# Attention in a decoder trunk: the products of probabilities and values in fp32r parts

## The chip, the core and the metric

The kernel runs on one core of a Trainium2 chip. The metric is the device time of one execution in microseconds, the median over runs. A core has five engines, each of which takes its own instructions in order: TensorE (PE in the profile, with its weight loads as PEld), VectorE (DVE), ScalarE (ACT), GpSimd (POOL), and SyncE (SP), which here only issues DMAs. They wait for one another through semaphores. Operands lie in SBUF; matmuls write into PSUM banks, from which VectorE and ScalarE read.

## The reference

Two layers on a sequence of 1024 positions of width 1024, all in fp32. Layer 0 ("even") has a mixer of two parts, a chunked gMLP and an attention with 8 heads of 64 channels; layer 1 has a gated linear attention; each layer ends with a gated MLP with a causal convolution. The change lies in the attention of layer 0, of which the kernel computes two branches: a causal band of the 128 positions before a query (window 128, dilation 1), and queries and keys strided by 4, with the third branch (dilation 16) folded into the masks of the second. Cut to what matters:

```python
def dilated_branch(q, k, v, window, dilation):      # blocks of 128 positions of one residue
    ...
    s = jnp.einsum('bhrnic,bhrnjc->bhrnij', qb, kk) * (hd ** -0.5)
    s = jnp.where(valid, s, NEG)
    m = jnp.max(s, -1, keepdims=True)
    p = jnp.exp(s - m)
    den = jnp.sum(p, -1)
    o = jnp.einsum('bhrnij,bhrnjc->bhrnic', p, vv) / den[..., None]
    lse = m[..., 0] + jnp.log(den)
```

The branches are then weighted by a softmax over their `lse`, and heads are put side by side.

## The kernel before

**Numbers.** TensorE multiplies in two formats here: fp32, and fp32r, a rounded form of it. For most products the kernel splits each fp32 operand into two fp32r parts, the rounded value (high) and the rest (low), and adds three products of parts. `split` (L98) makes the parts: ScalarE casts the high one (L100), VectorE subtracts it from the source for the low one (L101). `scaled` (L103) does the same with a factor on the source (L105, L106). The products of probabilities and values are plain fp32 matmuls in this kernel.

**The even mixer** starts with the transposed, split input `hq`, which all projections read. The attention runs in four passes of two heads each (`p` = 0 to 3). `project` (L694) does for each of eight tiles of 128 positions (`n`): the projection to queries, keys and values (24 matmuls of 384 columns into a bank `pj`, of which there are two), norms of queries and keys (VectorE, ScalarE, GpSimd), the scaled values `vN` (L718, ScalarE; three buffers), which also go to DRAM (`vd`), the transposes of the queries (`tq`) and keys (`tk`) with their copies, and then one `unit` (L668) of the first branch. Behind the eight tiles the values are read back in strided order (`v4`). `dilated` (L755) does eight such units on strided queries and keys (a quarter of the positions each, in two blocks).

A **unit** handles one block of 128 queries, two heads `s`, and one or two blocks `j` of keys. For each head: scores in a bank `sc` (L659, fp32r), the mask and the extremum in one VectorE instruction (L664), the exponential on ScalarE (L665), and a transpose of each block of probabilities on TensorE into a bank `pts` (L679). Then all blocks are copied to SBUF (`pT`), on ScalarE in odd units (L682) and on VectorE in even ones (L684), and multiplied by the values into `po` (L687):

```python
            for s in range(2):
                for j in range(nj):
                    T.matmul(po[:, i, 64 * s : 64 * s + 64], pT[:, s, j, :], vb[j][:, 64 * s : 64 * s + 64],
                             start=(j == 0), stop=(j == nj - 1))
```

`po` is one bank that takes four units, 128 columns each, and is then copied to `ot` by ScalarE (L747, L766). `combine` and `combined` weigh the branches by VectorE and GpSimd.

**Order.** Instructions are placed engine by engine by a scheduler at build time, which moves them across tiles and passes: the strided units of one pass stand among the projections of the next, and the gMLP's value and gate projections (`pv`, `pu`) among those of the last. Which instruction waits for which follows from buffers: a tile's buffer is reused when its last reader is done.

**Weights.** The projection's weights come as raw fp32 rows and are split into parts (`load_qkv`, L565), eight tiles to a pass. Passes 0 and 2 take four of them from a pool of their own, `wx`, with four buffers, and four from the pool `wp` with eight, which all other stages use too; passes 1 and 3 take all eight from `wp`.

Of the kernel before, what the change touches and what calls it, by code (L numbers as in the profile page):

```python
# [9 lines left out]
F32 = mybir.dt.float32  # L10
# [45 lines left out]
def trunk(ctx: ExitStack, tc: tile.TileContext, a, out):  # L56
# [452 lines left out]
    def even(gm_open):  # L509
        with ExitStack() as st:  # L510
# [6 lines left out]
            par0 = ExitStack()  # L517
            wx = par0.enter_context(tc.tile_pool(name="wx", bufs=4, side="right", reuse_waits="tile"))
            pq0 = par0.enter_context(tc.tile_pool(name="pq0", bufs=1, side="right", reuse_waits="tile"))
# [45 lines left out]
    def load_qkv(p, wx):  # L565

        ws = []
        for kp in range(4):
            raw = load_raw(a["w_qkv"][p, kp], f"wq{p}{kp}r", 768)
            for i in range(2):  # L570
                k = 2 * kp + i
                src, gain = raw[:, i * 384 : i * 384 + 384], g0[:, k : k + 1]
                if p % 2 or k >= 4:
                    ws.append(parts_of(src, f"wq{p}{kp}_{i}", gain=gain))
                else:
                    w = wx.tile([P, 2, 384], F32R, tag="wx", name=f"wx{p}{k}")
                    ws.append([w[:, j, :] for j in range(2)])
                    scaled(ws[-1], src, gain)
        return ws
# [61 lines left out]
    def attention(ps, at, av, pq, pq0, par0, wx, wq0, masks, gm_open):  # L641
# [26 lines left out]
        def unit(p, name, i, ot, po, qv, kv, vb, mask, wide=lambda t: t):  # L668


            nj = len(vb)
            W = nj * P
            pts = ps.tile([P, 2, nj, P], F32, tag="pt", name="pP" + name)
            for s in range(2):
                sm = scores(p, f"{name}{s}", qv(s), lambda part: kv(s, part), W,
                            mask[:, 2 * P - W :],
                            ot[:, i, 128 + s : 129 + s], ot[:, i, 130 + s : 131 + s], wide)
                for j in range(nj):
                    T.transpose(pts[:, s, j, :], sm[:, j * P : j * P + P], ident)  # L679
            pT = at.tile([P, 2, 2, P], F32, tag="pT", name="pT" + name)  # L680
            if i % 2:
                A.copy(pT[:, :, :nj, :], pts)  # L682
            else:
                V.tensor_copy(pT[:, :, :nj, :], pts)  # L684
            for s in range(2):
                for j in range(nj):
                    T.matmul(po[:, i, 64 * s : 64 * s + 64], pT[:, s, j, :], vb[j][:, 64 * s : 64 * s + 64],  # L687
                             start=(j == 0), stop=(j == nj - 1))

        def outputs(name):  # L690
            return (at.tile([P, 4, 132], F32, tag="ot", name="ot" + name, bufs=5),
                    ps.tile([P, 4, P], F32, tag="po", name="po" + name))

        def project(p, ws=None, then=None):  # L694
# [5 lines left out]
            kT = pool.tile([P, 4, S], F32R, tag="kT", bufs=1, name=f"kT{p}")  # L700
            vd = dram.tile([S, P], F32, name=f"vd{p}")
            vN, os = [], []
            for n in range(NT):
# [12 lines left out]
                G.tensor_tensor(qn, qn, gqk, op=ALU.mult)  # L716
                vN.append(pq.tile([P, P], F32, tag="vN", bufs=3, name=f"vN{p}{n}"))
                A.mul(vN[n], pj[:, 256:384], rn)  # L718
                Q.dma_start(rows(vd, n), vN[n])
                qs = pq.tile([P, 2, P], F32R, tag="qs", bufs=2, name=f"qs{p}{n}")  # L720
# [18 lines left out]
                if n % 4 == 0:  # L739
                    ot, po = outputs(f"{p}n{n}")  # L740
                    os.append(ot)
                m0 = max(n - 1, 0)
                unit(p, f"{p}n{n}", n % 4, ot, po, lambda s, qT=qT: qT[:, s],
                     lambda s, i: kT[:, 2 * s + i, :].rearrange("p (r m) -> p r m", r=4)[:, :, 32 * m0 : 32 * n + 32],
                     vN[m0 : n + 1], mband, lambda t: t.rearrange("p (m r) -> p r m", r=4))
                if n % 4 == 3:
                    A.copy(ot[:, :, :P], po)  # L747
                if then and n in (3, 4):
                    then(n - 3)
            v4 = av.tile([P, 4, 2, P], F32, tag="v4", name=f"v4{p}", bufs=1)  # L750
            for b in range(2):
                Q.dma_start(v4[:, :, b, :], vd.rearrange("(b m r) c -> b m r c", b=2, r=4)[b])
            return os, qR, kT, v4

        def dilated(p, qR, kT, v4):  # L755

            od = dram.tile([S, 132], F32, name=f"od{p}")
            for g in range(2):
                ot, po = outputs(f"{p}d{g}")
                for i in range(4):  # L760
                    r, b = 2 * g + i // 2, i % 2
                    at0 = r * 256
                    unit(p, f"{p}d{g}{i}", i, ot, po, lambda s: qR[:, s, at0 + b * P : at0 + b * P + P],
                         lambda s, part: kT[:, 2 * s + part, at0 : at0 + b * P + P],
                         [v4[:, r, j, :] for j in range(b + 1)], mboth)
                A.copy(ot[:, :, :P], po)  # L766
                for b in range(2):
                    Q.dma_start(od.rearrange("(b m r) c -> b m r c", b=2, r=4)[b][:, 2 * g : 2 * g + 2, :],
                                ot.rearrange("p (r b) c -> p r b c", b=2)[:, :, b, :])
# [508 lines left out]
```

## Time and profile before

| | us |
|---|---|
| median of three runs | 2185.39 |
| lowest and highest run | 2182.70, 2185.51 |
| the profiled execution | 2186.67 |
| its span, first to last instruction | 2185.0 |
| of that, to the first matmuls of the output projection (the even mixer) | 388.7 |
| granted TensorE clock, mean over the span | 0.996 |

A line of a view that groups instructions reads: line of the kernel, engine, operation, output <- inputs by the program's names, shape, number of instructions | busy time and mean duration in ns | idle time of the engine just ahead of them, with what ended it. A line of a view by windows has, for each engine, its busy time in that stretch and the number of instructions in brackets, then the granted clock, the DMA engines' busy share and what they moved. In a timeline a line is a run of like instructions: start and length in us, engine, instruction, count. An operation whose line is a helper's is told apart by its tile.

### The profile page before, as it was taken

To read this page: it belongs to the slowest core of one execution; us is meant where nothing else is said; L and a number is where in the kernel's file an instruction comes from. 1 tells how busy PE (TensorE), PEld (TensorE's weight loads), DVE (VectorE), ACT (ScalarE), POOL (GpSimd) and SP (SyncE) were. 2 spreads that over 40 slices of the span, in tenths; PEclk is the share of its full clock that TensorE was granted. 3 is DMA by queue.
4 is the path that set the end of the run, shared out by engine and by line. 5 is a ranking of instruction groups with operands and counts; after the bars stand their busy time and mean duration, and the time that the engine had idled before them with its cause. 6 is when DMAs were issued, how large, how long until landed. Compare 5 with 4: busy or idle time off the path is not lost.

```text
span 2185.0 us, 29867 instructions
## 1 busy us (share of the span) xinstructions
PE 2145.9 (98%) x10508; PEld 1817.9 (83%) x10508; DVE 1538.2 (70%) x2459; ACT 1032.7 (47%) x1998; POOL 488.4 (22%) x519
## 2 busy tenths in 40 slices
PE   8999999999999999999999999999999999999999
PEld 7999988778888888888889887878788888888887
DVE  6566655567888888755576777666787879885554
ACT  6455545355444444444454455524544444444443
POOL 4444411013242434100010011100233524320000
PEclk9999999999999999999999999999999999999999
DMA  4122212655445444675553222377544444557555
GB/s 162 43 81 63 73 50 83 217 198 194 162 155 164 158 165 159 196 271 198 196 202 123 68 97 97 116 265 248 193 160 150 158 159 159 164 178 271 204 196 202
DMA packets 157254, 349.59 MB, mean 160 GB/s; under 512 B 17408, under 2 KB 54272, under 8 KB 156720
## 3 DMA queue, kind: packets, MB, share of 16 engines
q1 hardware_dynamic: 157104, 347.68, 47.5%
q8 instruction: 83, 1.36, 0.3%
q14 instruction: 67, 0.55, 0.1%
HBM read 239.02 MB, written 108.59 MB: 159 GB/s over the span
## 4 chain that ended last, share of the span: by engine, by line
PE 70%; DMA 4%; DVE 3%; ACT 1%; issue 1%; SPq 0%; POOL 0%; DVEq 0%; ACTq 0%
PE puB L290 11%; PE pgB L290 11%; PE pgC L290 5%; PE puC L290 5%; PE pdB L397 5%; PE pdC L397 5%; PE pv L190 4%; PE pdO L397 4%; PE puA L290 3%; PE pgA L290 3%; PE po L190 2%; PE pdQ L397 2%; PE pdP L397 2%; PE pBq L990 2%; PE pBr L990 2%
## 5 line engine op out<-in xcount | busy, mean ns | idle before, releaser
L101 DVE TENSOR_TENSOR da<-ar,da 128x512 fp32r<-128x512 f32 x154 | 106.4, 691 | 155.3 <-ACT da L100 155.2
L100 ACT CAST da<-ar 128x512 fp32r<-128x512 f32 x154 | 95.9, 622 | 209.4 <-PE pdC L397 91.3
L190 PE MATMUL po<-wo,hq 128*128 128x512 f32 x768 | 186.4, 398 | 0.6 <-DVE hq L101 0.3
L190 PEld LDWEIGHTS po<-wo,hq 128*128 128x128 f32 x768 | 143.3, 190 | 30.9 <-DVE hq L101 1.2
L190 PE MATMUL pv<-wv,hq 128*128 128x512 f32 (+2 forms) x768 | 139.9, 340 | 2.1 <-DVE b L1022 1.6
L397 PE MATMUL pdB<-dw,da 128*128 128x512 f32 x528 | 136.3, 391 | 0.6 <-ACT dw L100 0.6
L397 PE MATMUL pdC<-dw,da 128*128 128x512 f32 x528 | 135.9, 390 | 0.0
L190 PEld LDWEIGHTS pv<-wv,hq 128*128 128x128 f32 x768 | 119.0, 189 | 17.4 <-DVE b L1022 2.1
L190 PE MATMUL pj<-wq,hq 128*128 128x384 f32 x576 | 118.1, 348 | 0.0
L397 PEld LDWEIGHTS pdB<-dw,da 128*128 128x128 f32 x528 | 98.7, 188 | 21.9 <-ACT dw L100 1.0
L397 PEld LDWEIGHTS pdC<-dw,da 128*128 128x128 f32 x528 | 99.1, 188 | 20.4
L256 POOL TENSOR_TENSOR S1g<-rg 128x512 f32<-128x512 f32 x20 | 29.6, 1480 | 381.2 <-DMA wsd<-D 326.9
L101 DVE TENSOR_TENSOR dw<-wr,dw 128x512 fp32r<-128x512 f32 x154 | 105.9, 687 | 11.2 <-ACT dw L100 11.1
L140 POOL TENSOR_SCALAR rn<-ssq 128x1 f32<-128x1 f32 x24 | 8.1, 337 | 470.1 <-ACT h L148 245.6
L397 PE MATMUL pdO<-dw,da 128*128 128x512 f32 x396 | 102.3, 390 | 0.2 <-DVE dw L101 0.2
L100 ACT CAST dw<-wr 128x512 fp32r<-128x512 f32 x154 | 95.0, 617 | 15.0 <-DMA wr<-in_w_dn 7.6
L190 PEld LDWEIGHTS pj<-wq,hq 128*128 128x128 f32 x576 | 101.0, 192 | 0.4 <-ACT vN L718 0.2
L397 PEld LDWEIGHTS pdO<-dw,da 128*128 128x128 f32 x396 | 74.3, 188 | 15.9 <-DVE dw L101 0.6
L319 DVE SCALAR_TENSOR_TENSOR t<-g,cw,t 128x1022 f32<-128x1022 f32 x44 | 76.7, 1742 | 0.1
L318 DVE SCALAR_TENSOR_TENSOR t<-g,cw,t 128x1023 f32<-128x1023 f32 x44 | 59.4, 1350 | 16.5 <-ACT t L317 16.5
L303 DVE TENSOR_TENSOR g<-g,s1g 128x512 f32<-128x512 f32 x22 | 16.2, 738 | 77.1 <-ACT s1g L302 77.1
L320 ACT ACTIVATE t<-t 128x1024 f32<-128x1024 f32 x44 | 46.7, 1061 | 32.7 <-DVE t L319 32.7
(1073 smaller groups left out, 5478.7 us busy)
## 6 DMA issues: line engine op xcount, KB each, us to landing
ar<-actd SPq DMA_DIRECT2D x70, 512.0 KB, 3.5
rd<-in_w_down SPq DMA_DIRECT2D x44, 512.0 KB, 3.6
wsd<-D SPq DMA_DIRECT2D x88, 256.0 KB, 2.4
rg<-in_w_gate SPq DMA_DIRECT2D x42, 512.0 KB, 3.6
ru<-in_w_up SPq DMA_DIRECT2D x42, 512.0 KB, 4.8
wr<-wsd SPq DMA_DIRECT2D x40, 512.0 KB, 4.4
actd<-t SPq DMA_DIRECT2D x66, 256.0 KB, 2.2
wr<-in_w_dn SPq DMA_DIRECT2D x30, 512.0 KB, 4.9
```

What stands on the lines that cost most here:

```text
L100: (hi or A.copy)(dst[0], src)
L101: (lo or V.tensor_sub)(dst[1], src, f32(dst[0]))
L140: G.tensor_scalar(r, ssq, 1.0 / n, EPS, op0=ALU.mult, op1=ALU.add)
L190: T.matmul(o, L[i], R[jj][:, sl], start=(k == 0 and (ii, jj) == PASSES[0]), stop=(k == nk - 1 and (ii, jj) == PASSES[-1]))
L256: G.tensor_tensor(sums[name], x, y, op=op)
L290: T.matmul(o, L[ii][:, j * P : j * P + P], right[p][:, jj, j, :], skip_group_check=more, start=(not more and j == 0 and (ii, jj) == PASSES ...
L303: V.tensor_add(C22, C22, s1)
L318: V.scalar_tensor_tensor(t[:, 1:], g[:, : S - 1], w(1), t[:, 1:], op0=ALU.mult, op1=ALU.add)
L319: V.scalar_tensor_tensor(t[:, 2:], g[:, : S - 2], w(0), t[:, 2:], op0=ALU.mult, op1=ALU.add)
L320: A.activation(t, t, AF.Silu)
L397: T.matmul(o, L[ii][:, t * P : t * P + P], R[jj], skip_group_check=more, start=start and not more and (ii, jj) == PASSES[0], stop=stop and ...
L990: T.matmul(o, L[ii][:, j * P : j * P + P], right[p][:, jj, j, :], skip_group_check=more, start=(not more and j == 0 and (ii, jj) == PASSES ...
```

## The change

Probabilities are written as two fp32r parts (`pT` doubles, `split`), values too (`vN`, `vd` and `v4` double; `scaled` in the place of the scaling on ScalarE). For each head and block, the high part of the probabilities meets the high and the low values side by side in one matmul of 128 columns, and the low part meets the high values in one of 64. The two halves of the accumulator are added as it is emptied: ScalarE copies the half that got both high-value products, VectorE adds the other. The accumulator takes two units instead of four (still one bank). `wx` has three buffers instead of four, so that passes 0 and 2 take five of the eight weight tiles from `wp`.

```diff
@@ -515,7 +515,7 @@
             pq = st.enter_context(tc.tile_pool(name="pq", bufs=1, reuse_waits="tile"))
             masks = band_masks(pq)
             par0 = ExitStack()
-            wx = par0.enter_context(tc.tile_pool(name="wx", bufs=4, side="right", reuse_waits="tile"))
+            wx = par0.enter_context(tc.tile_pool(name="wx", bufs=3, side="right", reuse_waits="tile"))
             pq0 = par0.enter_context(tc.tile_pool(name="pq0", bufs=1, side="right", reuse_waits="tile"))
             with tc.tile_pool(name="nrm", bufs=1, reuse_waits="tile") as pool:
                 for n in range(NT):
@@ -570,7 +570,7 @@
             for i in range(2):
                 k = 2 * kp + i
                 src, gain = raw[:, i * 384 : i * 384 + 384], g0[:, k : k + 1]
-                if p % 2 or k >= 4:
+                if p % 2 or k >= 3:
                     ws.append(parts_of(src, f"wq{p}{kp}_{i}", gain=gain))
                 else:
                     w = wx.tile([P, 2, 384], F32R, tag="wx", name=f"wx{p}{k}")
@@ -677,19 +677,23 @@
                             ot[:, i, 128 + s : 129 + s], ot[:, i, 130 + s : 131 + s], wide)
                 for j in range(nj):
                     T.transpose(pts[:, s, j, :], sm[:, j * P : j * P + P], ident)
-            pT = at.tile([P, 2, 2, P], F32, tag="pT", name="pT" + name)
+            pT = at.tile([P, 2, 2, 2, P], F32R, tag="pT", name="pT" + name)
+            split([pT[:, part, :, :nj, :] for part in range(2)], pts)
+            for s in range(2):
+                o = po[:, i % 2, s]
+                for j in range(nj):
+                    T.matmul(o, pT[:, 0, s, j, :], vb[j][:, s], start=(j == 0), stop=False)
+                    T.matmul(o[:, :64], pT[:, 1, s, j, :], vb[j][:, s, :64], start=False, stop=(j == nj - 1))
             if i % 2:
-                A.copy(pT[:, :, :nj, :], pts)
-            else:
-                V.tensor_copy(pT[:, :, :nj, :], pts)
-            for s in range(2):
-                for j in range(nj):
-                    T.matmul(po[:, i, 64 * s : 64 * s + 64], pT[:, s, j, :], vb[j][:, 64 * s : 64 * s + 64],
-                             start=(j == 0), stop=(j == nj - 1))
+                o = ot[:, i - 1 : i + 1, :P].rearrange("p i (s c) -> p i s c", s=2)
+                A.copy(o, po[:, :, :, :64])
+                V.tensor_add(o, o, po[:, :, :, 64:])
 
         def outputs(name):
-            return (at.tile([P, 4, 132], F32, tag="ot", name="ot" + name, bufs=5),
-                    ps.tile([P, 4, P], F32, tag="po", name="po" + name))
+            return at.tile([P, 4, 132], F32, tag="ot", name="ot" + name, bufs=5)
+
+        def halfway(name):
+            return ps.tile([P, 2, 2, P], F32, tag="po", name="po" + name)
 
         def project(p, ws=None, then=None):
 
@@ -698,7 +702,7 @@
             pool = pq if p % 2 else pq0
             qR = pool.tile([P, 2, S], F32R, tag="qR", bufs=1, name=f"qR{p}")
             kT = pool.tile([P, 4, S], F32R, tag="kT", bufs=1, name=f"kT{p}")
-            vd = dram.tile([S, P], F32, name=f"vd{p}")
+            vd = dram.tile([S, 2 * P], F32, name=f"vd{p}")
             vN, os = [], []
             for n in range(NT):
                 pj = ps.tile([P, 512], F32, tag="pj", name=f"pj{p}{n}")
@@ -714,9 +718,9 @@
                 V.scalar_tensor_tensor(heads(qn), heads(pj[:, :256]), rn, r[:, :, None].to_broadcast([P, 4, 64]),
                                        op0=ALU.mult, op1=ALU.mult)
                 G.tensor_tensor(qn, qn, gqk, op=ALU.mult)
-                vN.append(pq.tile([P, P], F32, tag="vN", bufs=3, name=f"vN{p}{n}"))
-                A.mul(vN[n], pj[:, 256:384], rn)
-                Q.dma_start(rows(vd, n), vN[n])
+                vN.append(pq.tile([P, 2, P], F32R, tag="vN", bufs=3, name=f"vN{p}{n}"))
+                scaled([vN[n][:, :, :64], vN[n][:, :, 64:]], heads(pj[:, 256:384]), rn)
+                Q.dma_start(rows(vd, n), f32(flat(vN[n])))
                 qs = pq.tile([P, 2, P], F32R, tag="qs", bufs=2, name=f"qs{p}{n}")
                 ks = pq.tile([P, 4, P], F32R, tag="ks", bufs=2, name=f"ks{p}{n}")
                 split([qs[:, :, :64], qs[:, :, 64:]], heads(qn[:, :P]), hi=G.tensor_copy)
@@ -737,33 +741,34 @@
                 (V.tensor_copy if n % 2 else A.copy)(four(kT), by4(f32(tk)))
 
                 if n % 4 == 0:
-                    ot, po = outputs(f"{p}n{n}")
+                    ot = outputs(f"{p}n{n}")
                     os.append(ot)
+                if n % 2 == 0:
+                    po = halfway(f"{p}n{n}")
                 m0 = max(n - 1, 0)
                 unit(p, f"{p}n{n}", n % 4, ot, po, lambda s, qT=qT: qT[:, s],
                      lambda s, i: kT[:, 2 * s + i, :].rearrange("p (r m) -> p r m", r=4)[:, :, 32 * m0 : 32 * n + 32],
                      vN[m0 : n + 1], mband, lambda t: t.rearrange("p (m r) -> p r m", r=4))
-                if n % 4 == 3:
-                    A.copy(ot[:, :, :P], po)
                 if then and n in (3, 4):
                     then(n - 3)
-            v4 = av.tile([P, 4, 2, P], F32, tag="v4", name=f"v4{p}", bufs=1)
+            v4 = av.tile([P, 4, 2, 2, P], F32R, tag="v4", name=f"v4{p}", bufs=1)
             for b in range(2):
-                Q.dma_start(v4[:, :, b, :], vd.rearrange("(b m r) c -> b m r c", b=2, r=4)[b])
+                Q.dma_start(f32(v4[:, :, b].rearrange("p r s c -> p r (s c)")), vd.rearrange("(b m r) c -> b m r c", b=2, r=4)[b])
             return os, qR, kT, v4
 
         def dilated(p, qR, kT, v4):
 
             od = dram.tile([S, 132], F32, name=f"od{p}")
             for g in range(2):
-                ot, po = outputs(f"{p}d{g}")
+                ot = outputs(f"{p}d{g}")
                 for i in range(4):
+                    if i % 2 == 0:
+                        po = halfway(f"{p}d{g}{i}")
                     r, b = 2 * g + i // 2, i % 2
                     at0 = r * 256
                     unit(p, f"{p}d{g}{i}", i, ot, po, lambda s: qR[:, s, at0 + b * P : at0 + b * P + P],
                          lambda s, part: kT[:, 2 * s + part, at0 : at0 + b * P + P],
-                         [v4[:, r, j, :] for j in range(b + 1)], mboth)
-                A.copy(ot[:, :, :P], po)
+                         [v4[:, r, j] for j in range(b + 1)], mboth)
                 for b in range(2):
                     Q.dma_start(od.rearrange("(b m r) c -> b m r c", b=2, r=4)[b][:, 2 * g : 2 * g + 2, :],
                                 ot.rearrange("p (r b) c -> p r b c", b=2)[:, :, b, :])
```

## The prediction

> **What bounds the kernel now.** I read the page first: which engine carries the span, and which line the chain that ended last runs through.
>
> ```profile
> span 2185.0 us, 29867 instructions
> ...
> PE 2145.9 (98%) x10508; PEld 1817.9 (83%) x10508; DVE 1538.2 (70%) x2459; ACT 1032.7 (47%) x1998; POOL 488.4 (22%) x519
> ...
> PE 70%; DMA 4%; DVE 3%; ACT 1%; issue 1%; SPq 0%; POOL 0%; DVEq 0%; ACTq 0%
> ```
>
> TensorE is busy almost throughout, and the chain is TensorE's own work. An edit therefore pays only if it shortens TensorE's stream, and costs only where it makes TensorE wait. Next I cut the span into stretches: the even mixer (0 to 388.7 us, all that the change touches), the rest, and inside the mixer one whole pass, pass 1, in three pieces: its first tiles, the rest of its projection, and the strided units.
>
> ```profile
> core 0: us, PE busy (x) PEld busy (x) DVE busy (x) ACT busy (x) POOL busy (x), PEclk, DMA share, GB/s
> 112.80:124.00 11.20, 10.67 (x92) 9.75 (x91) 9.23 (x33) 9.15 (x32) 2.66 (x5) 1.00 0.33 84
> 124.00:155.90 31.90, 30.56 (x199) 29.00 (x198) 22.37 (x59) 13.83 (x36) 17.23 (x25) 1.00 0.34 103
> 155.90:180.00 24.10, 24.10 (x182) 23.98 (x181) 12.46 (x48) 14.40 (x49) 10.93 (x21) 1.00 0.06 16
> 112.80:180.00 67.20, 65.33 (x469) 62.73 (x467) 44.06 (x137) 37.38 (x115) 30.82 (x51) 1.00 0.24 68
> 180.00:246.30 66.30, 64.99 (x468) 62.84 (x466) 41.54 (x132) 35.18 (x112) 29.59 (x51) 1.00 0.20 57
> 45.50:48.90 3.40, 3.40 (x20) 3.40 (x20) 2.18 (x9) 2.75 (x10) 1.91 (x4) 0.50 0.02 5
> 69.40:76.20 6.80, 6.77 (x24) 6.58 (x24) 3.60 (x9) 0.37 (x1) 2.56 (x5) 0.50 0.44 138
> 0.00:388.70 388.70, 372.12 (x2353) 344.75 (x2354) 234.39 (x659) 213.27 (x544) 137.67 (x242) 0.99 0.27 84
> ```
>
> A pass takes about 67 us, with TensorE full, VectorE at 44.1 (66%) and ScalarE at 37.4 (56%). The tightest piece is the first: from 112.8 to 124.0 VectorE is busy 9.23 of 11.20 us. Behind 388.7 us each engine's instructions stand in the same order in both kernels, so that part moves as a whole; the forecast is the change of the first 388.7 us.
>
> **Does TensorE's stream get shorter?** One product of probabilities and values was an fp32 matmul of 64 columns; it becomes an fp32r matmul of 128 columns and one of 64. The rows give what each costs in a stream:
>
> ```profile
> L687 PE MATMUL po1n<-vN,pT1n 128*128 128x64 f32 x60 | 7.7, 271 | 0.0
> L687 PEld LDWEIGHTS po1n<-vN,pT1n 128*128 128x128 f32 x60 | 7.5, 191 | 0.1
> L659 PEld LDWEIGHTS sc1d<-kT,qR 128*128 128x128 f32 x32 | 4.9, 191 | 0.0
> L679 PE MATMUL pP1n<-ident,sm1n 128*128 128x128 f32 x30 | 5.8, 281 | 0.5 <-ACT sm1n L665 0.5
> ...
> 148.05 0.97 PEld L687 LDWEIGHTS po1n<-vN,pT1n 128*128 128x128 f32 x8
> ...
> 148.05 1.10 PE L687 MATMUL po1n<-vN,pT1n 128*128 128x64 f32 x8
> ...
> 155.91 0.56 PE L659 MATMUL sc1d<-kT,qR 128*128 128x128 f32 x4
> 156.47 2.37 PE L190 MATMUL pj<-wx,hq 128*128 128x384 f32 x12
> ```
>
> A projection pass transposes 30 blocks (pP1n x30), so it has 30 products, but 60 records: an fp32 product is already two weight loads and two matmuls. With the 24 of the strided units (four residues, one and two blocks, two heads) that is 54 products a pass, 216 in four passes, 432 records before and 432 matmuls after. The load of an fp32 tile and of an fp32r tile last the same (191 ns in both load rows). In a run of eight the fp32 loads follow one another at (0.97 - 0.19) / 7 = 0.111 us, the matmuls at (1.10 - 0.27) / 7 = 0.118; four fp32r matmuls of 128 columns follow at (0.56 - 0.22) / 3 = 0.113, with 0.22 estimated for the last of them, near the shortest 128-column matmul. Both are the pace of the load, not of the columns: at the 384-column pace, (2.37 - 0.34) / 11 = 0.185 us, or 0.48 ns a column, 64 columns need 0.03 us and 128 need 0.06. So 432 x 0.115 becomes 432 x 0.113: 0.9 us less, and nothing below the load's pace to be had. I take -1; the bounds are 0 and -2.
>
> The Trainium skill counts otherwise ("FP8 and Floating Point Precision", "TensorE Precision Notes": true FP32 is four passes through the array). By that count the change trades 4 x 64 columns for 192. The trace shows two records for a product, both paced by the load; the count matters only if columns set the pace, which is the third rival.
>
> **What is added beside TensorE.** Prices by the nearest rows:
>
> ```profile
> L101 DVE TENSOR_TENSOR hq<-pt,hq 128x512 fp32r<-128x512 f32 x16 | 11.0, 686 | 9.7 <-ACT hq L100 9.7
> L101 DVE TENSOR_TENSOR ks<-qn,ks 128x256 fp32r<-128x256 f32 x32 | 15.3, 478 | 0.0
> L101 DVE TENSOR_TENSOR qs<-qn,qs 128x128 fp32r<-128x128 f32 x32 | 13.8, 433 | 8.7 <-POOL qs L100 8.6
> L664 DVE CUSTOM_DVE_ANT_1 sm1n<-sc1n,mband 128x256 f32<-128x256 f32 x14 | 8.5, 624 | 5.1 <-PE sc1n L659 4.4 <-PE pP1n L679 0.6
> L684 DVE COPY pT1n<-pP1n 128x512 f32<-128x512 f32 x3 | 2.1, 689 | 1.0 <-PE pP1n L679 1.0
> L682 ACT COPY pT1n<-pP1n 128x512 f32<-128x512 f32 x4 | 2.3, 580 | 2.3 <-PE pP1n L679 2.2
> L731 ACT CAST qT<-tq 128x256 fp32r<-128x256 f32 x32 | 11.8, 368 | 10.4 <-PE tq L728 9.3 <-PE sc3n L659 0.3 <-PE sc2n L659 0.3
> L718 ACT ACTIVATE vN<-pj,r 128x128 f32<-128x128 f32 x32 | 11.4, 358 | 20.1 <-PE po0n L687 9.9 <-DVE qn L714 9.9 <-PE po1n L687 0.2
> L766 ACT COPY ot1d<-po1d 128x512 f32<-128x512 f32 x2 | 1.1, 564 | 0.0
> ```
>
> Per pass. Probabilities: each of the 16 units now needs a high part on ScalarE and a low part on VectorE, where odd units had a ScalarE copy and even ones a VectorE copy. VectorE gains eight subtractions of 512 elements, 8 x 0.69 = 5.5 us; on even units it trades a copy (0.69) for a subtraction (0.69), +0. ScalarE gains three casts of 512 and five of 256, 3 x 0.58 + 5 x 0.37 = 3.6. Values: eight low parts of 128, 8 x 0.43 = 3.5 on VectorE; the high part takes the scaling's place. Outputs: the accumulator is emptied every two units instead of four, and its low half added: eight adds of 256 on VectorE, 8 x 0.48 = 3.8; on ScalarE eight copies of 256 for four of 512, 8 x 0.37 - 4 x 0.56 = +0.7. VectorE +12.8, to 57 of 67.2 us (85%); ScalarE +4.3, to 42 (62%). Neither total passes TensorE's, so on average all of it is hidden, and the question is the pieces.
>
> **The piece where it isn't hidden.** In the changed kernel's order for pass 1, TensorE runs from the first score of tile 0 to the projection of tile 5 through 81 matmuls and transposes without one projection matmul between them (92 records in the row of the first piece, a few projections at its end among them). That projection needs a bank that is free only when tile 3's value low part is done on VectorE. In VectorE's own order this low part now stands behind the scores of tiles 0 to 4 and everything between: 8 score reductions of 256 (8 x 0.62) and 2 of 128 (0.4 each), 3 low parts of 512 (0.69) and 2 of 256 (0.48), 2 output adds (0.48), the key copy (0.69), the query scaling (0.48), query and key low parts (0.43 and 0.48), and itself (0.43): 5.0 + 0.8 + 2.1 + 1.0 + 1.0 + 0.7 + 0.5 + 0.9 + 0.4 = 12.4 us. TensorE's 81 are 81 x 0.113 = 9.2 us. Before, the same stretch is the 112.80:124.00 row: 9.23 us of VectorE in 11.20, and the projection waited only for ScalarE's scaling. So VectorE, in order, sets the stretch: 12.4 plus the gap until its first score arrives, about 0.7 (an estimate: the row before keeps 2 us of VectorE idle in this stretch, and a longer queue leaves less of it), 13.1 against 11.2: +1.9. Queued behind that low part are the output adds and the next tiles' norms, queued behind the projection all of TensorE.
>
> In the rest of the projection, VectorE had 22.4 of 31.9 us; a good half of the added 12.8 lands there, and it runs at about 90%: each late score costs TensorE some tenths; I put +1 a pass. The strided units have 12.5 of 24.1: +0. So +2.9 a pass. The order of passes 0 and 2 has the same dense first tiles; in pass 3 the scores of tile 4 come only behind that projection, two score reductions less ahead of it (1.2 us), and the later tiles stand among value projections: +1. Sum: 3 x 2.9 + 1 - 1 = +9, rounded. Bounds: nothing (all in VectorE's idle time) and twice that, +17, if the idle gaps of the stretch don't close up (2 us a pass more).
>
> **Edits that cost nothing.** The value rows double in size, 32 stores and 8 strided loads on SyncE's queue, in the same number:
>
> ```profile
> vd<-vN SPq DMA_DIRECT2D x32, 64.0 KB, 1.5
> v<-vd SPq DMA_DIRECT2D x8, 256.0 KB, 3.1
> ...
> 151.62 0.52 SPq L752 DMA_DIRECT2D v<-vd  x1
> ...
> L687 PE MATMUL po1d<-v,pT1d x48: 217/275/324, 167.2 to 184.1; 128*128 128x64 f32 x48
> ```
>
> The last load of pass 1 is issued at 151.6 and first used at 167.2: 15.6 us of cover for 3.1, or at most 6.2 if the time doubles. One weight tile fewer has its own slot, so five instead of four wait at a pass change for the pass before; the strided units fill that time, and without them it would be one more pair of casts of 384 elements, about 1.1 us by the rows of 256 and 512 (0.5 on ScalarE, 0.6 on VectorE), at a few places; I take 0.
>
> **The rivals.**
> *It is hidden after all.* For it: 85% is not full, and the order is made anew. Against it: the stretch counted above. Sum: -1 + 0 to 5, a time of 2184 to 2189, which is no change.
> *VectorE becomes the bound and TensorE's clock drops.* The rows at 45.5 and 69.4 show the granted clock at 0.50 for 3.4 and 6.8 us, both in pass 0. If the new waits, some 3 to 4 us in 13, do the same once in each of passes 0 to 2, that is 3 x 3.4 at half clock, 5 us lost, beside the forecast's +9 at least and +17 at most: +14 to +22, 2199 to 2207. [...]
> *TensorE's stream does get shorter, and the kernel faster.* If columns, not loads, set the pace where loads are pulled ahead under wide matmuls, 64 columns fewer for each of 216 products are worth 64 x 0.48 ns x 216 = 6.6 us; and the new order may close gaps: pass 1 lost 67.2 - 65.3 = 1.9 us of plain idle time, four passes some 8. Both together with the stretch unharmed: -5 to -13, 2172 to 2180. It decides where TensorE's load lane has idle time around the products; against it stand 23.98 of 24.10 us of busy loads in the strided units, and the 0.113.
>
> **The numbers.** The profiled execution took 2186.67 us around its 2185.0; the median of the runs is 2185.39, 1.3 less. 2186.7 + 9 - 1.3 gives 2194.4. Chances: forecast (+4.4 to +14) 0.52, bound and clock 0.16, hidden 0.20, shorter 0.12. 0.2% is 4.4 us, about what a measurement of this kernel can tell from no change: slower 0.68, same 0.20, faster 0.12. The range, 2182 to 2207, leaves out the faster case and reaches the end of the slowest; the forecast's own part of it is 2190 to 2199.
>
> **What would show it.** Right: as many TensorE records in the mixer as before, products still at 0.11 us; VectorE some 50 us busier in the mixer; in passes 0 to 2 a wait of TensorE for VectorE's value low part (the helper's scaled subtraction into vN) ahead of tile 5's projection; output work starting at about 398 instead of 388.7 us, and the rest as long as before, 1796 us. Wrong: products well under 0.11 us; a pass at or under 67 us; a change behind the mixer; or TensorE waits that name ScalarE or a DMA of the values.

## The result, and the profile after

The changed kernel takes 2219.36 us (median of four runs, 2212.12 to 2223.95) against 2185.42 of the kernel before on the same chip: a ratio of 1.0141, 95% interval [1.0119, 1.0162], slower by 34 us between the medians, by 26 to 35 within the interval. The prediction had the direction, not the size: 2194.4, range 2182 to 2207. The profiled execution took 2223.95 us around a span of 2222.2, 37.3 more than the one of before: of the four executions two took 2212.12 and 2215.06 us at a mean granted clock of 0.993, two 2223.65 and 2223.95 at 0.988, and the profile is of one of the latter. The head of its page:

```profile
span 2222.2 us, 30077 instructions
...
PE 2165.4 (97%) x10508; PEld 1833.1 (82%) x10508; DVE 1570.3 (71%) x2555; ACT 1048.1 (47%) x2044; POOL 485.9 (22%) x519
...
PE 71%; DMA 4%; DVE 2%; ACT 1%; issue 1%; POOL 0%; SPq 0%; DVEq 0%; ACTq 0%
```

TensorE has the 10508 matmul records that it had before, and carries the chain as before; in the totals nothing but 20 us more of its busy time shows. The stretches tell more. The changed kernel cut as the prediction cut the one before: mixer, rest, the first stretch of pass 1, passes 1 and 2.

```profile
core 0: us, PE busy (x) PEld busy (x) DVE busy (x) ACT busy (x) POOL busy (x), PEclk, DMA share, GB/s
0.00:424.10 424.10, 390.92 (x2353) 360.80 (x2354) 270.04 (x755) 227.16 (x590) 136.50 (x242) 0.94 0.27 86
424.10:2222.20 1798.10, 1774.46 (x8156) 1472.32 (x8155) 1300.22 (x1801) 820.89 (x1455) 349.37 (x277) 1.00 0.52 177
117.50:128.90 11.40, 9.87 (x83) 8.82 (x81) 10.58 (x35) 10.33 (x35) 3.72 (x7) 1.00 0.09 25
117.50:192.10 74.60, 68.87 (x470) 66.17 (x468) 52.02 (x159) 42.05 (x127) 29.13 (x50) 0.95 0.24 74
192.10:271.50 79.40, 73.71 (x476) 71.01 (x475) 51.25 (x160) 40.42 (x124) 29.35 (x50) 0.89 0.22 68
```

The mixer went from 388.7 to 424.1 us, +35.4; the rest is as long as before. The first row against its row of before splits the loss in two: TensorE's idle time grew from 388.70 - 372.12 = 16.6 to 424.10 - 390.92 = 33.2, **+16.6 us of waits**; its busy time grew by **18.8 us over the same 2353 records**, at a granted clock of 0.94 instead of 0.99. The same in the passes: pass 2 is 13.1 us longer, 4.4 of it idle (5.69 for 1.31) and 8.7 busy.

**The waits.** The first row below is the longest sum among TensorE's waits in the mixer, the second the longest among VectorE's; the kernel before has neither. Then two rows of the view that groups instructions, the values' high part (ScalarE) and low part (VectorE).

```profile
PE pj L190 <- DVE vN L106: 7.8, 8, 1.8
...
DVE vN L106 <- ACT vN L105: 21.4, 13, 4.6
```

```profile
L105 ACT ACTIVATE vN<-pj,r 128x128 fp32r<-128x128 f32 x32 | 11.6, 363 | 28.2 <-DVE qn L718 11.4 <-PE po3n L686 4.9 <-PE po2n L686 4.2
L106 DVE SCALAR_TENSOR_TENSOR vN<-pj,r,vN 128x128 fp32r<-128x128 f32 x32 | 11.1, 348 | 21.4 <-ACT vN L105 21.4
```

TensorE waits for a projection bank, which VectorE's low part frees; VectorE stands still for ScalarE's high part; ScalarE waits for products (`po`, L686) for 16.5 of its 28.2 us, 10.1 before: one of the three `vN` tiles must be read out before it can be written. All of TensorE's waits in the mixer that name the low part are 8.8 us, half of the 16.6; the largest increases beside them are the key copies in VectorE's queue (4.4 for 0.8) and the low part of `hq` (3.9 for 1.6). The timeline of pass 1 has one turn of that wheel, on TensorE, ScalarE, VectorE and TensorE again:

```profile
128.92 3.59 PE L190 MATMUL pj<-wq,hq 128*128 128x384 f32 x19 [1.10 <-DVE vN L106]
...
132.37 0.31 PE L685 MATMUL po1n<-vN,pT1n 128*128 128x128 f32 x1
132.51 0.24 PE L686 MATMUL po1n<-vN,pT1n 128*128 128x64 f32 x1
132.59 0.30 PE L685 MATMUL po1n<-vN,pT1n 128*128 128x128 f32 x1
...
133.94 0.30 PE L685 MATMUL po1n<-vN,pT1n 128*128 128x128 f32 x1
...
133.24 0.37 ACT L105 ACTIVATE vN<-pj,r 128x128 fp32r<-128x128 f32 x1 [3.77 <-PE po1n L686]
...
133.64 0.35 DVE L106 SCALAR_TENSOR_TENSOR vN<-pj,r,vN 128x128 fp32r<-128x128 f32 x1 [3.85 <-ACT vN L105]
...
142.06 0.34 DVE L106 SCALAR_TENSOR_TENSOR vN<-pj,r,vN 128x128 fp32r<-128x128 f32 x1
...
142.46 0.79 PE L190 MATMUL pj<-wq,hq 128*128 128x384 f32 x3 [1.82 <-DVE vN L106]
```

TensorE begins with a wait for the bank, the one that the prediction had placed ahead of tile 5's projection, of 1.10 us. The products at 132.4 stand behind the 19 projection matmuls in its queue. Until they have read the tile, ScalarE stands for 3.77 us, and VectorE, behind it, for 3.85. Then VectorE works off what has gathered, the weighing of the branches of pass 0 among it (135.1 to 142); the next low part comes at 142.06, and TensorE has waited 1.82 us for its bank.

The product rows also show the pace of the pairs, a first and an eighth among them: (133.94 - 132.37) / 7 = 0.224 us a pair, 0.112 a matmul, as forecast.

**The clock.** Stretches at half clock in the mixer, each with the 3.4 us ahead of it; the last two rows are the same places in the kernel before, ahead of its two.

```profile
140.50:143.90 3.40, 1.58 (x9) 1.45 (x9) 3.20 (x6) 1.09 (x3) 2.29 (x5) 1.00 0.23 67
143.90:147.30 3.40, 3.40 (x13) 3.40 (x12) 3.17 (x7) 2.37 (x4) 0.98 (x2) 0.50 0.80 239
195.10:198.50 3.40, 2.56 (x20) 2.20 (x20) 3.40 (x12) 2.23 (x9) 1.40 (x4) 1.00 0.01 2
198.50:201.90 3.40, 3.40 (x21) 3.40 (x19) 2.74 (x9) 2.13 (x8) 0.66 (x1) 0.50 0.28 79
229.30:232.70 3.40, 2.09 (x15) 1.46 (x13) 2.80 (x8) 1.76 (x5) 2.71 (x6) 0.99 0.15 59
232.70:242.90 10.20, 9.81 (x43) 9.21 (x42) 5.93 (x16) 5.45 (x17) 3.11 (x6) 0.50 0.10 27
304.40:307.80 3.40, 0.67 (x6) 0.67 (x6) 3.40 (x8) 0.18 (x1) 1.41 (x3) 0.99 0.74 211
```

```profile
42.10:45.50 3.40, 1.91 (x13) 1.63 (x14) 3.40 (x12) 2.62 (x8) 1.86 (x3) 1.00 0.00 0
66.00:69.40 3.40, 1.86 (x16) 1.47 (x13) 3.40 (x7) 2.50 (x6) 2.73 (x4) 1.00 0.68 207
```

There are nine such stretches in the mixer instead of two, 47.8 us (14 steps of 3.41) instead of 10.2. A projection matmul of 384 columns lasts 685 ns in the median inside them and 336 outside, so the work takes twice its time there, and 37.6 us more of it cost 18.8, as in the sum. TensorE had been idle for 0.84 to 2.73 us of the 3.4 ahead of each.

### The profile page after: what moved, and what is told of

It is laid out like the page before. It is cut to its first block, busy times and chain, and to the rows that moved or that the text cites. A ratio compares the mean times of both kernels' runs of the same rounds, so it can differ in the third digit from the quotient of the medians.

```text
span 2222.2 us, 30077 instructions
## 1 busy us (share of the span) xinstructions
PE 2165.4 (97%) x10508; PEld 1833.1 (82%) x10508; DVE 1570.3 (71%) x2555; ACT 1048.1 (47%) x2044; POOL 485.9 (22%) x519
## 4 chain that ended last, share of the span: by engine, by line
PE 71%; DMA 4%; DVE 2%; ACT 1%; issue 1%; POOL 0%; SPq 0%; DVEq 0%; ACTq 0%
PE puB L290 11%; PE pgB L290 11%; PE pgC L290 5%; PE puC L290 5%; PE pdB L397 5%; PE pdC L397 5%; PE po L190 4%; PE pv L190 4%; PE pdO L397 4%; PE puA L290 3%; PE pgA L290 2%; PE pdQ L397 2%; PE pdP L397 2%; PE pBq L995 2%; PE pBr L995 2%; DMA xd<-xt 1%
## 5 line engine op out<-in xcount | busy, mean ns | idle before, releaser
L190 PE MATMUL pj<-wq,hq 128*128 128x384 f32 x624 | 138.8, 361 | 4.9 <-DVE vN L106 4.9
L190 PEld LDWEIGHTS pj<-wq,hq 128*128 128x128 f32 x624 | 114.9, 202 | 6.0 <-DVE vN L106 4.7
L397 PEld LDWEIGHTS pdC<-dw,da 128*128 128x128 f32 x528 | 99.1, 188 | 20.5
L101 DVE TENSOR_TENSOR dw<-wr,dw 128x512 fp32r<-128x512 f32 x154 | 105.8, 687 | 10.2 <-ACT dw L100 10.0
L318 DVE SCALAR_TENSOR_TENSOR t<-g,cw,t 128x1023 f32<-128x1023 f32 x44 | 58.4, 1327 | 16.6 <-ACT t L317 16.6
```

What stands on the lines that cost most here:

```text
L101: (lo or V.tensor_sub)(dst[1], src, f32(dst[0]))
L190: T.matmul(o, L[i], R[jj][:, sl], start=(k == 0 and (ii, jj) == PASSES[0]), stop=(k == nk - 1 and (ii, jj) == PASSES[-1]))
L318: V.scalar_tensor_tensor(t[:, 1:], g[:, : S - 1], w(1), t[:, 1:], op0=ALU.mult, op1=ALU.add)
L397: T.matmul(o, L[ii][:, t * P : t * P + P], R[jj], skip_group_check=more, start=start and not more and (ii, jj) == PASSES[0], stop=stop and ...
```

## The experiments

Three theories. A: VectorE's place in the hand-over of the projection's bank makes it late, and TensorE with it. B: VectorE simply has too much to do. C: the new products and accumulators, or the new order, cost by themselves. Every edit but one makes the order of instructions anew, so each result holds a change of order too; e13 alone has the order of the changed kernel, instruction for instruction. The table gives for each kernel the median, the ratio to the kernel before on the same chip with its interval, and from the profiled run the mixer's length, TensorE's idle and busy time in it (2352 or 2353 records throughout), and VectorE's busy time in it, all in us.

| kernel | median | ratio | mixer | PE idle | PE busy | DVE busy |
|---|---|---|---|---|---|---|
| before | 2185.4 | 1 | 388.4 | 16.6 | 371.8 | 234 |
| changed | 2219.4 | 1.0141 [1.0119, 1.0162] | 423.9 | 33.2 | 390.7 | 270 |
| e1: before, weight slots | 2186.3 | 1.0002 [0.9992, 1.0011] | 385.2 | 16.9 | 368.3 | 233 |
| e2: changed, no value low part | 2201.0 | 1.0072 [1.0053, 1.0091] | 400.6 | 23.7 | 376.9 | 261 |
| e3: changed, no probability low part | 2206.9 | 1.0094 [1.0079, 1.0109] | 402.8 | 27.8 | 375.0 | 236 |
| e4: changed, no output add | 2204.8 | 1.0088 [1.0072, 1.0105] | 404.3 | 26.8 | 377.5 | 261 |
| e5: before + load | 2195.7 | 1.0052 [1.0037, 1.0067] | 395.4 | 25.3 | 370.1 | 273 |
| e6: before + split values | 2203.2 | 1.0083 [1.0068, 1.0098] | 399.9 | 26.8 | 373.1 | 240 |
| e7: changed, none of the three | 2183.6 | 0.9991 [0.9977, 1.0004] | 383.5 | 16.1 | 367.4 | 219 |
| e8: before, five value tiles | 2177.3 | 0.9972 [0.9958, 0.9986] | 378.9 | 13.9 | 365.0 | 229 |
| e10: e6, five value tiles | 2184.3 | 0.9991 [0.9979, 1.0003] | 381.5 | 17.4 | 364.2 | 238 |
| e11: e5, five value tiles | 2185.0 | 1.0000 [0.9987, 1.0013] | 386.4 | 17.8 | 368.6 | 271 |
| e12: changed, values by way of SBUF | 2186.8 | 1.0003 [0.9989, 1.0017] | 389.4 | 17.5 | 371.9 | 264 |
| e13: changed, four `ut` tiles | 2218.1 | 1.0137 [1.0112, 1.0161] | 413.9 | 32.0 | 381.9 | 271 |
| e14: e13, four value tiles | 2197.6 | 1.0051 [1.0033, 1.0069] | 399.1 | 24.9 | 374.2 | 268 |

### One part at a time: e1 to e4

e1, in the kernel before:

```diff
-wx = ... tc.tile_pool(name="wx", bufs=4, ...)      -if p % 2 or k >= 4:
+wx = ... tc.tile_pool(name="wx", bufs=3, ...)      +if p % 2 or k >= 3:
```

> The kernel before with the weight slots of the change alone: three own slots instead of four, five tiles from the common pool in passes 0 and 2. Slots matter: one more pair of casts is late at each pass change, 1 to 2 us each, so 2188 to 2193. Slots don't matter (my prediction took 0): 2183 to 2188.

2186.3, no difference: the weight slots cost nothing. In the changed kernel, e2, e3 and e4:

```diff
-scaled([vN[n][:, :, :64], vN[n][:, :, 64:]], heads(pj[:, 256:384]), rn)
+A.activation(vN[n] as (s, 2, 64), heads(pj[:, 256:384]) twice, AF.Copy, scale=rn)     # e2
...
-split([pT[:, part, :, :nj, :] for part in range(2)], pts)
+A.copy(pT[:, 0, :, :nj, :], pts)                       # e3, and pT[:, 0] in the second matmul
...
-V.tensor_add(o, o, po[:, :, :, 64:])                   # e4
```

> The changed kernel without the low part of the values: ScalarE writes the high part into both halves, VectorE has no work on the values and no part in freeing the projection's bank (the output leaves out the low values). Everything else, TensorE's stream above all, stays. Theory A, VectorE's queue holds the projection's bank and stands still behind the values: nearly all of the stalls and with them the half-clock stretches go, 2188 to 2198. Theory B, sheer load of VectorE: 32 of some 100 added instructions and 11 of 36 us go, so about a third of the 34 us, 2205 to 2212. Theory C, the hand-over of the two-unit accumulator: no change, 2212 to 2224.

> The changed kernel without the low part of the probabilities: the 64 subtractions are not made and the second matmul takes the high part again (the output leaves out the low probabilities), so TensorE's stream is the same. It takes away some 39 us of VectorE's work, more than any other edit. Theory A: the values' wait stays, 2205 to 2218. Theory B: VectorE is back near its load of before, 2188 to 2196. Theory C: 2212 to 2224.

> The changed kernel without the 32 additions of the accumulator's low half (the output leaves out the products with the low values); ScalarE's copy alone frees the accumulator. Theory A: 2210 to 2220. Theory B: 13 us of VectorE's work less, a third, 2205 to 2212. Theory C, the hand-over through two engines every two units holds TensorE: 2188 to 2200.

Each gives back 12 to 18 of the 34 us, 45 together, and none all: the parts don't add up. Of the three only e3 came where a theory had put it, A (2205 to 2218); e2 with 2201.0 lies between the ranges of A and B, e4 with 2204.8 just under B's and further under A's. VectorE's busy time doesn't tell which gives most. e2 spares it 9 us of 270 and gives back 18; e3 spares it 34 and gives back 12, and VectorE still stands for ScalarE's value, 25.7 us in the mixer. That speaks for a wait and against load, but settles neither: in e2 the bank is ScalarE's to free, and nearly 16 us of the loss stay. e4 fits A worst: ScalarE waits only 3.5 us for products there and TensorE 2.7 for the low part, and yet 19 us of the loss stay: 10 us more idle time than before, in many small waits, and 6 more busy. What they come from, the new order included, was not tested.

### The suspects one by one: e5 to e8

e5, e6 and e8 start from the kernel before, e7 from the changed one:

```diff
+V.tensor_add(junk, <pT, as 512>, sum512)      # e5: 512 in odd units, 256 in every second, 128 a tile
...
-A.mul(vN[n], pj[:, 256:384], rn)              # e6, vd and v4 of double size, products read the high part, three slots of wx as in e1
+scaled([vN[n][:, :, :64], vN[n][:, :, 64:]], heads(pj[:, 256:384]), rn)
...
                                               # e7: the edits of e2, e3 and e4 together
...
-vN.append(pq.tile([P, P], F32, tag="vN", bufs=3, ...))
+vN.append(pq.tile([P, P], F32, tag="vN", bufs=5, ...))       # e8
```

> The kernel before, with VectorE made busier by about as much as the change makes it (a pass more by some 8 additions of 512, 8 of 256 and 8 of 128 elements, all of them reading from and writing to SBUF, with no reader of what they write): nothing of TensorE or ScalarE waits for one of them, but they stand in VectorE's queue among the rest. If sheer VectorE load is the cause (theory B), most of the 34 us return: 2205 to 2220, with half-clock stretches in passes 0 to 2. If the cause is that a projection bank is handed back through VectorE (theory A), the time stays within 10 us of before, 2185 to 2195, and VectorE names no wait over 2 us in all at the projection.

> The kernel before with the values alone split: high part on ScalarE, low part on VectorE straight out of the projection's bank, stored and loaded at double size; probabilities and products stay as they were, and the products read the high part alone. VectorE gains 8 low parts of 128 elements a pass (3.5 us), a quarter of the change's additions. Theory A: the hand-over alone makes VectorE stand behind ScalarE's value and TensorE behind VectorE's: 2195 to 2206, half of the change's loss, with a VectorE wait named ScalarE's value of over 5 us. Theory B: a quarter of the load brings under a quarter of the loss, 2185 to 2193.

> The changed kernel without any of VectorE's three additions: the values' low part isn't made (ScalarE writes the high part into both halves), the probabilities' low part isn't made (the high part is used in its place), the accumulator's low half isn't added. TensorE's records, loads, columns and DMAs stay those of the change. If all of the loss is VectorE's (A and B alike), 2183 to 2190. If the new products, the two-unit accumulators or the new order hold a part of it themselves (theory C), 2195 or more.

> The kernel before with five value tiles in place of three. Before, ScalarE's scaling of the values waits 9.9 us in the mixer for products that still read the tile; TensorE waits for little of it. All theories: within 4 us of before (2181 to 2187); under 2180 would say that ScalarE's wait for a value tile costs time already in the kernel before, and that the change's loss begins at that wait.

The mixers of e5 and e7, by windows:

```profile
0.00:395.40 395.40, 370.09 (x2352) 341.18 (x2352) 272.96 (x757) 213.22 (x544) 146.73 (x242) 1.00 0.26 80
```

```profile
0.00:383.50 383.50, 367.41 (x2352) 339.81 (x2352) 219.13 (x628) 229.07 (x592) 138.65 (x242) 1.00 0.29 91
```

e5 keeps VectorE as busy as the change does (273 us for 270) and costs 10 us, at a granted clock of 1.00. Load (B) isn't the 34, though it isn't nothing, and 10 us just misses the bound that A had given. Nor is e5 load alone: its additions of 512 read what ScalarE has just written, and VectorE stands 13.0 us for that in the mixer. e6, with a quarter of the additions, costs 17.5, as A said, and its VectorE stands behind ScalarE's value as in the change (from 30 to 390 us):

```profile
DVE vN L106 <- ACT vN L105: 17.5, 10, 3.5
```

e7 has the changed kernel's products, accumulators and transfers, and is as fast as before: C falls, and TensorE's new stream is neither shorter nor longer as far as the medians tell. (VectorE is busy for 15 us less than in the kernel before; by e5's price, 10 us for 39, that could hide some 4 us.) In e7 ScalarE waits for products as long as in the change, 16.6 us for 16.5, and nothing is lost: the wait costs by what hangs on it. e8 missed what all theories gave: two more value tiles make the kernel before 8 us faster. So the number of value tiles mattered already, and the change's loss had to be looked for there. (What in e8 gained is less sure: its scaling still waits 6.7 us for products, 9.9 before, so the new order may have a part in it.)

### The tile and the bank: e10 to e14

e10 and e11 are e6 and e5 with five value tiles. The other three start from the changed kernel; for the room in SBUF each has four tiles instead of five for `ut`, a product in the prologue. Five value tiles in the changed kernel (e9), the direct counterpart of e8, need more SBUF than there is even so (the pool of `v4` takes 8 kb a partition, 7.09 were left). So there is no time for that kernel, for which A gave 2185 to 2195; e14 has four.

```diff
-scaled([vN[n][:, :, :64], vN[n][:, :, 64:]], heads(pj[:, 256:384]), rn)      # e12
+vS = pq.tile([P, P], F32, tag="vS", bufs=2, ...)
+A.mul(vS, pj[:, 256:384], rn)
+split([vN[n][:, :, :64], vN[n][:, :, 64:]], heads(vS), hi=G.tensor_copy)
...
-t = gm.tile([P, 512], F32, tag="ut", bufs=5, ...)
+t = gm.tile([P, 512], F32, tag="ut", bufs=4, ...)                            # e12, e13, e14
...
-vN.append(pq.tile([P, 2, P], F32R, tag="vN", bufs=3, ...))
+vN.append(pq.tile([P, 2, P], F32R, tag="vN", bufs=4, ...))                   # e14
```

> The kernel before with the values alone split, as in the run that took 2203, and five value tiles. Theory A, sharpened: the price of the hand-over falls from 17.5 us to under 8, against 2177 of the kernel before with five tiles: 2178 to 2185. If the hand-over through VectorE costs by itself, the 17.5 us stay: 2192 to 2197.

> The kernel before with the added VectorE load that nothing waits for, and five value tiles. With three tiles the load cost 10 us, and TensorE's largest wait was for ScalarE's value. If that too went through the tile, 2177 to 2182. If a fuller VectorE queue costs by itself, 2184 to 2190.

> The changed kernel with the values scaled into a tile of SBUF by ScalarE first, which frees the projection's bank; GpSimd casts the high part, VectorE subtracts from that tile, so VectorE's work stays as it is, with three value tiles (and four ut tiles for the room). The scaling no longer waits for a value tile. If the bank's hand-over is what costs (theory A), about as without the values' low part (2201): 2198 to 2206, no wait of TensorE for the value at the projection. If VectorE's queue standing still behind the value is what costs, whoever frees the bank, 2210 or more, with VectorE's wait for the value (then GpSimd's) still over 10 us.

> The changed kernel with four tiles in place of five for the prologue's product ut, and nothing else: the room that the run over SBUF took. If ut has no part in it, as both theories have it, the time is that of the changed kernel within its spread, 2210 to 2226. Under 2205 would say that the run over SBUF was cured in part by the tile count or by a new order, not by the bank.

> The changed kernel, the hand-over through VectorE kept, with four value tiles in place of three (and four ut tiles for the room). If the loss is the wait for a value tile, one tile more takes most of it: 2185 to 2200, VectorE's wait for ScalarE's value at 10 us or less in the mixer. If a bank freed by VectorE costs by itself, 2205 or more, and that wait stays near 20 us.

With five tiles the hand-over through VectorE costs 2184.3 - 2177.3 = 7 us instead of 17.5 (e10, inside A's figure); the load costs 7.6 instead of 10 (e11, as a fuller queue would, not by way of the tile). The strongest result is e12: 2186.8, below the ranges of both theories. Its mixer, and the group rows of its scaling and low part:

```profile
0.00:389.40 389.40, 371.91 (x2353) 345.48 (x2353) 264.21 (x755) 227.22 (x592) 144.90 (x274) 0.99 0.30 94
```

```profile
L101 DVE TENSOR_TENSOR vN<-vS,vN 128x128 fp32r<-128x128 f32 x32 | 12.0, 378 | 1.7 <-POOL vN L100 1.7
L723 ACT ACTIVATE vS<-pj,r 128x128 f32<-128x128 f32 x32 | 11.7, 365 | 11.0 <-DVE qn L718 10.0 <-DVE vN L101 1.1
```

VectorE has as many instructions as in the change (755) and nearly its busy time, but the scaling waits for no product any more, VectorE's 21.4 us of standing behind the value are 1.7, TensorE's wait for the value is gone, and so are the 32 us. A had counted the bank alone, and expected e2's time. In e2, too, ScalarE frees the bank, but only after 16.0 us of waits for products; it is 14 us slower, with less for VectorE to do. The wait for the tile has gone to GpSimd's queue, 19.1 us over the four passes, where no bank hangs on it:

```profile
POOL vN L100 <- PE po0n L686: 5.6, 5, 2.0
```

e13 shows that `ut` has no part in that (2218.1). It shows the clock's part, too. Its mixer has the change's order and its idle time (32.0 us for 33.2), but only 23.9 us at half clock for 47.8; it has 8.8 us less of busy time and is 10 us shorter. e14 shows that the hand-over through VectorE may stay: one value tile more takes 20.5 of e13's 32 us away. The time is as A said, the sum beside it is not: between 30 and 390 us VectorE still waits 16.1 us for the value (10 or less expected; 19.5 in e13), and TensorE's waits that name the low part are 7.9 us (8.3 in e13). The wait for the tile did shrink: ScalarE's waits for products ahead of the value are 5.8 us, 16.0 in e13. What has gone for TensorE are its waits for other things in VectorE's queue, the key copies first, and some clock: 24.9 us idle and 374.2 busy, for 32.0 and 381.9. The waits of e13 and those of e14, ScalarE's for products behind TensorE's:

```profile
PE pj L190 <- DVE vN L106: 8.3, 8, 1.8
PE sc3n L659 <- DVE kT L741: 3.1, 1, 3.1
...
PE sc1n L659 <- DVE kT L741: 2.0, 1, 2.0
...
  ACT vN L105: 16.0, 5
```

```profile
PE pj L190 <- DVE vN L106: 4.1, 5, 2.0
PE pv L190 <- DVE vN L106: 3.8, 1, 3.8
...
  ACT vN L105: 5.8, 4
```

**The account.** More value tiles are worth 8 us to the kernel before and 11 to the one with load (e8, e11), where ScalarE frees the bank; 19 and 20.5 to those where VectorE frees it behind ScalarE (e10, e14). Load without the hand-over costs 8 to 10 us (e5, e11; e12 stands 9 above e8). So, as an estimate from these differences, of the change's 34 us some 9 are load, and the greater part, some 25, is the hand-over meeting too few tiles: with the tile's wait taken out of it, e12 is level with the kernel before. The differences are good to about 4 us each, and they hold the orders of different builds. That the hand-over and the tiles matter is shown in three ways (e6 and e10, e12, e13 and e14); the split is not, since "load" holds VectorE's standing behind ScalarE (e5), and e4 is 19 us slower than the kernel before with little of either wait.

The version that beats both kernels is e8: 2177.3, a ratio of 0.9972 [0.9958, 0.9986] to the kernel before. Its gain has nothing to do with the parts of the probabilities and values. The fastest kernel with all that the change computes is e12, level with the kernel before.

## Why the prediction was wrong

**TensorE's stream: right.** The records are the same 2353, a product 0.224 us a pair where 2 x 0.113 was forecast, and e7 is level with before.

**VectorE's addition: too large.** Some 50 us were forecast for the mixer, 270.04 - 234.39 = 35.6 came; ScalarE got 13.9 of 17. The prices were durations of one instruction, and in a queue without gaps they overlap: added one by one, VectorE's durations grew by 43.7 us, from 270.7 to 314.4. The low part and the add took 0.35 and 0.42 us, too, not 0.43 and 0.48.

**The first stretch: the right wait, too large.** TensorE does wait there for VectorE's low part, but 11.4 us were measured where the sum gave 13.1 and the kernel before had 11.2: VectorE was busy for 10.58 of them where 12.4 had been counted. +0.2 instead of +1.9. (The stretch holds 83 TensorE records, the one of before 92; its idle time went from 0.53 to 1.53 us.)

**The rest of the projection: the term that failed on the waits.** "Each late score costs TensorE some tenths; I put +1 a pass." The largest waits aren't late scores, they are the bank again, later in the pass: idle time grew by 3.9 us in pass 1, 1.0 of it in the first stretch, and by 4.4 in pass 2, and the waits that name the low part are 2.9 and 3.1 us there. The forecast asked how long VectorE's queue is and took it as always moving. It stands, for up to 4.6 us at a time, behind an instruction of ScalarE that waits for a tile. The sign of it stood in a row that the prediction quoted for its price alone: ScalarE's scaling, idle for 20.1 us, "<-PE po0n L687 9.9". A wait that the change puts a second engine and a bank behind should have been followed up. As a sum the waits stayed inside the forecast's bounds, +16.6 where +17 was the upper end; that is luck in part, since the first stretch was priced too high and the rest too low.

**The clock: the term that failed on the size.** The forecast's sum had no term for it, the rival 5 us, "3 x 3.4 at half clock"; it was 18.8 in the profiled execution; in e13's, of the same order, it was (23.9 - 10.2) / 2 = 6.8. The rival named the mechanism of the clock; its count was wrong: "once in each of passes 0 to 2" was nine times in all, up to 10.2 us in one piece, behind 0.84 to 2.73 us of idle time in the 3.4 ahead. Its other half did not come: VectorE is not the bound, with 52.0 of pass 1's 74.6 us. The traces of before could have told of the clock: ahead of its two half-clock stretches TensorE was idle for only 3.40 - 1.91 = 1.5 us. That waits bring the clock down is read from these rows; no run set the clock by itself. But the two fall together: e12 is back at 17.5 us idle and 371.9 busy. How much of it an execution meets varies, as e13 and the change show with one order.

**Weights, transfers, the rest: right.** e1 is level, the doubled values' loads took 3.8 us where 15.6 of cover had been counted, and what follows the mixer took 1798.1 us for 1796.3. The wrong sign that the prediction named, TensorE waiting for ScalarE or a DMA of the values, did not come: the wait named VectorE, which stood behind ScalarE.

## What to carry to other kernels

When a step that frees a PSUM bank is split over two engines, look first at what the first of them waits for: a row of idle time that cost little so far becomes a wait of the second engine, of everything queued on it, and of TensorE. Take the data out of the bank into a tile that nobody else holds, and do the rest from there (32 us here), or give the shared tile one buffer more (20 us here; the kernel before gained 8). And price each wait of TensorE twice, for itself and for the half-clock stretch that can follow it.

## What the runs showed of the hardware

The clock fell after little idle time, and not always after the same. Ahead of half-clock stretches stand windows with 0.84 us idle of 3.4 (the row at 195.10) and up to 2.73; others, with 1.07 and 1.58 us, were followed by full clock, in the changed kernel and in the one before:

```profile
201.90:205.30 3.40, 2.33 (x20) 2.09 (x19) 2.46 (x8) 3.32 (x10) 0.00 (x0) 0.99 0.53 120
```

```profile
21.60:25.00 3.40, 1.82 (x16) 1.55 (x14) 2.49 (x6) 2.73 (x6) 2.60 (x5) 1.00 0.89 299
25.00:28.40 3.40, 3.40 (x21) 3.40 (x21) 1.90 (x5) 1.58 (x5) 3.01 (x7) 1.00 0.39 143
```

The starts and lengths of the stretches lie on a grid of 3.41 us: 143.9, 198.5, 232.7 and 307.8 are 16, 10 and 22 steps apart. Cut along that grid from 20 us on, the fifteen profiles have 40 windows at full clock with over 2 us of TensorE idle time, and half clock followed each; it followed 31 of the 228 with 0.71 to 2 us, and none with less. What decides in between, these traces don't show. The Trainium skill ("TensorE: Matmul & The Clock Gate", "What's actually happening") has half rate begin after at least one idle window of some 3.4 us, in a window that runs freely. The grid and the length agree with the trace; the idle window does not: none of the nine was idle throughout, and 0.84 us of one was enough.
